# Attention: transposes in tiles of two banks, with the scores put between transposes and value products

## The chip, the core and the metric

The kernel runs on one core of a Trainium2 chip. The metric is the device time of one execution in microseconds. The engines are named as the profile names them: PE (TensorE, matrix products and transposes), DVE (VectorE), ACT (ScalarE), POOL (GpSimd) and SP (SyncE, which issues the DMAs).

## What is computed

One layer of an encoder: a combined input projection, RWKV-7 time mixing on half of the width, stick-breaking attention on the other half, an output projection and a squared-ReLU MLP. The change touches the attention alone:

```python
for blk in range(T // Q_BLOCK):
    z = jnp.einsum('bhqd,bhkd->bhqk', q[:, :, start:end], k[:, :, :end]) * scale
    causal = jnp.arange(end)[None, :] < (start + jnp.arange(Q_BLOCK))[:, None]
    log_beta = jax.nn.log_sigmoid(z)
    log_keep = jnp.where(causal, log_beta - z, 0.0)
    log_a = log_beta + lax.cumsum(log_keep, axis=3, reverse=True) - log_keep
    att = jnp.where(causal, jnp.exp(log_a), 0.0)
    outs.append(jnp.einsum('bhqk,bhkd->bhqd', att, v[:, :, :end]))
```

There are 2048 tokens and 8 attention heads of 64.

## The kernel before

The program runs three stages one after the other: projections with RWKV (stage 1), attention (stage 2), output projection with the MLP (stage 3). In stage 2 the queries stand in four blocks b of 512 and the heads in four pairs hp. For each pair of b and hp, key blocks j of 512 keys are gone through from j=b (the diagonal one) down to j=0. One such (b, hp, j) is a **step**: 40 steps, of which 16 are diagonal and 24 are full. A step has a front and a back.

- `front` (lines 262 to 284), once for each of four query tiles i: PE makes the scores z of both heads (L271; with a mask in a diagonal step, L273), ACT takes two sigmoids of them (`keep`, L275, and `ga`, L277), DVE scans `keep` backwards into E (L281, once for each head), POOL multiplies `ga` by E (L282). There are two z buffers (two PSUM banks each) and two `keep` buffers, nine of `ga` and six of E.
- `back` (lines 285 to 304), once for each of four key tiles kt: PE transposes the 128x128 pieces of `ga` into a PSUM tile `tr`, the tile is copied to SBUF as `th`, and the value products read `th` and add up in OT. A key tile is done in two halves u, of two query tiles each: four transposes into a `tr` of one bank (two buffers), one copy of 512 elements (ACT, L302, or for three of eight DVE, L301), two products (L304). In a diagonal step the pieces above the diagonal are left out.
- `finish` (lines 305 to 313), after the last step of a head pair: DVE copies OT, PE transposes it into `o` (L310, in a buffer of `tr`), ACT copies `o` out (L312) and a DMA stores it.

`step` (lines 316 to 326) issues the front of a new step and the back of the step before it, one tile of each in turn. What order the engines get is set by a scheduler when the program is built: it moves instructions past each other within these dependences, so that fronts can stand up to about a step and a half ahead. Each engine then works through its own list in order, and waits on semaphores.

Stage 3 loads its first data through SP's queue; these loads stand behind the store of the last `osb` (L313).

In names such as `th31210` or `ga3122` the digits are b, hp, j, then the tile, and in `th` and `tr` of the kernel before a last digit u.

Of the kernel before, what the change touches and what calls it, by code (L numbers as in the profile page):

```python
# [8 lines left out]
F32 = mybir.dt.float32  # L9
# [234 lines left out]
def stage2(tc,consts,kd,qd,vd,sbd,cfg=None):  # L244

    nc=tc.nc; V_=nc.vector; A=nc.scalar; P=nc.gpsimd; TE=nc.tensor
    g=dict(GA=9,E=6,TH=4,QB=3,DV=(1,4,7))
    g.update(cfg or {})
    with ExitStack() as ctx:
        sp=ctx.enter_context(tc.tile_pool(name="s2",bufs=1,reuse_waits="tile"))  # L250
# [34 lines left out]
        def back(b,hp,j,gas,OT,kt):  # L285

            n=f"{b}{hp}{j}"; V=kv[hp,j][1]
            i0=kt if j==b else 0; q0=128*i0
            for u in range(2):

                c0=max(i0,2*u)
                if c0>=2*u+2: continue
                tr=pt.tile([128,2,256],F32,tag="tr",name=f"tr{n}{kt}{u}",bufs=2)
                for h in range(2):
                    for i in range(c0,2*u+2):
                        ga,o=gas[i]
                        TE.transpose(tr[:,h,128*(i-2*u):128*(i-2*u)+128],ga[:,h,o+128*kt:o+128*kt+128],consts['ident'])  # L297
                th=sp.tile([128,2,256],F32,tag="th",name=f"th{n}{kt}{u}",bufs=g['TH'])
                q=slice(128*(c0-2*u),256); qq=slice(128*c0,256*u+256)
                cnt[1]+=1  # L300
                if cnt[1]%8 in g['DV']: V_.tensor_copy(out=th[:,:,q],in_=tr[:,:,q])  # L301
                else: A.copy(th[:,:,q],tr[:,:,q])  # L302
                for h in range(2):
                    TE.matmul(OT[64*h:64*h+64,qq],lhsT=V[:,kt,64*h:64*h+64],rhs=th[:,h,q],start=j==b and kt==0 and u==0,stop=j==0 and kt==3 and u==1,skip_group_check=True)  # L304
        def finish(b,hp,OT):
# [3 lines left out]
            o=pt.tile([128,4,128],F32,tag="tr",name="o"+n,bufs=2)  # L309
# [6 lines left out]
        def step(new):  # L316
            prev,late[0]=late[0],new
            for i in range(4):
                if new:
                    b,hp,j,Q,carry,gas,st=new  # L320
                    gas.append(front(b,hp,j,Q,carry,i))
                if prev:
                    b,hp,j,Q,carry,gas,st=prev
                    if j==b and i==0: st.append(pp.tile([128,512],F32,tag="OT",name=f"OT{b}{hp}",bufs=1))
                    back(b,hp,j,gas,st[0],i)
                    if j==0 and i==3: finish(b,hp,st[0])
# [403 lines left out]
```

## Time and profile before

| | us |
|---|---|
| median of 3 runs (3341.51 to 3344.73) | 3343.86 |
| the profiled execution | 3338.49 |
| its span, first to last instruction | 3336.7 |
| attention stage, 1122.9 to 1665.4 of the span | 542.5 |
| PE busy in it | 506.8 |
| DVE busy in it | 397.3 |
| ACT busy in it | 369.2 |
| POOL busy in it | 274.5 |

The page of the profile gives shares over the whole span, in which the attention is a sixth. So the views to read are those cut to this stage: busy time of the engines in a window, the waits of PE there, and the timeline, which shows in order what each engine did and how long it sat idle before. A busy time of PE counts the ends of its products, which run on while the next product starts; the distance between starts is what an instruction occupies.

### The profile page before, as it was taken

What the parts mean: (1) busy time and instruction counts of PE and PEld (TensorE: products, weight loads), DVE (VectorE), ACT (ScalarE), POOL (GpSimd) and SP (SyncE); (2) the same over time, 40 slices, a digit from 0 to 9 for tenths busy, and PEclk for the clock granted to TensorE, in tenths of its full rate; (3) what the DMA queues carried; (4) which work ended last, traced back from release to release, by engine and by line L of the source; (5) the groups of instructions that cost most, each with busy time, mean ns of one, the idle gap of its engine ahead of it and who ended that gap; (6) DMA issues with size and microseconds to landing.
All of it is one profiled execution on the core that took longest, in us unless ns stands there. A gap on an engine that the chain in (4) does not pass through costs nothing. (4 is left out here: it accounts for less than half of the span.)

```text
span 3336.7 us, 45433 instructions
## 1 busy us (share of the span) xinstructions
PE 3166.1 (95%) x17504; PEld 2398.0 (72%) x17504; DVE 2010.7 (60%) x3139; ACT 1167.7 (35%) x2192; POOL 1245.4 (37%) x1089
## 2 busy tenths in 40 slices
PE   8999999999998799999959999999999999999998
PEld 6677767777777544444448788888888888888887
DVE  4674575476375477778566555555555755555555
ACT  4434443443442476667522221111111411111112
POOL 5444444443442354555455432222222422222223
PEclk9999999999998799999979999999999999999999
DMA  3342242232232400000065221111111421111111
GB/s 100 101 120 74 85 131 75 83 121 83 73 100 66 136 23 17 14 10 7 4 199 165 89 76 51 51 45 45 45 51 48 158 79 51 51 45 45 44 44 63
DMA packets 146729, 239.30 MB, mean 72 GB/s; under 512 B 50000, under 2 KB 58192, under 8 KB 146512
## 3 DMA queue, kind: packets, MB, share of 16 engines
q1 hardware_dynamic: 146512, 236.39, 22.7%
q8 instruction: 138, 2.26, 0.3%
q14 instruction: 79, 0.65, 0.1%
HBM read 190.14 MB, written 46.20 MB: 71 GB/s over the span
## 5 line engine op out<-in xcount | busy, mean ns | idle before, releaser
L160 DVE TENSOR_TENSOR acc<-acc,dn 128x512 f32<-128x512 f32 x512 | 344.5, 685 | 411.2 <-PE dn L32 405.6
L282 POOL TENSOR_TENSOR ga<-ga,E 128x1024 f32<-128x1024 f32 (+3 forms) x160 | 274.5, 1726 | 275.6 <-ACT ga L277 124.5
L145 ACT ACTIVATE r<-up 128x512 f32<-128x512 f32 x128 | 75.6, 592 | 615.4 <-PE up L32 615.4
L148 DVE TENSOR_TENSOR m<-r 128x512 f32<-128x512 f32 x128 | 190.9, 1492 | 113.5 <-ACT r L145 113.5
L281 DVE TENSOR_TENSOR_SCAN E<-keep,E,pad 128x513 f32<-128x513 f32 x192 | 232.4, 1263 | 36.4 <-ACT keep L275 36.4
L304 PE MATMUL OT<-th,V 128*64 128x256 f32 (+1 forms) x1152 | 179.5, 392 | 18.2 <-DVE th L301 17.8
L297 PEld LDWEIGHTS tr<-ident,ga 128*128 128x128 f32 x1088 | 114.5, 140 | 105.6 <-issue 94.1
L297 PE MATMUL tr<-ident,ga 128*128 128x128 f32 x1088 | 181.5, 287 | 5.4 <-DVE th L301 2.2
L271 PE MATMUL z<-K,Q 64*128 64x512 f32 (+3 forms) x640 | 159.8, 582 | 11.4 <-DMA Q<-qd 7.7
L275 ACT ACTIVATE keep<-z 128x1024 f32<-128x1024 f32 (+3 forms) x160 | 144.7, 906 | 72.1 <-PE z L273 31.0
L149 DVE TENSOR_TENSOR gl<-m,gh 128x512 fp32r<-128x512 f32 x128 | 148.4, 1160 | 11.6 <-ACT gh L146 0.9
L277 ACT ACTIVATE ga<-z 128x1024 f32<-128x1024 f32 (+3 forms) x160 | 143.7, 904 | 29.1 <-PE tr L297 28.4
L304 PEld LDWEIGHTS OT<-th,V 128*64 128x64 f32 x1152 | 57.6, 134 | 103.4 <-issue 40.1
L302 ACT COPY th<-tr 128x512 f32<-128x512 f32 (+1 forms) x180 | 101.2, 566 | 75.8 <-PE tr L297 74.7
L386 POOL TENSOR_TENSOR wls<-wfs,whs 128x512 fp32r<-128x512 f32 x64 | 84.3, 1318 | 109.1 <-ACT whs L385 100.8
L281 DVE TENSOR_TENSOR_SCAN E<-keep,pad 128x129 f32<-128x129 f32 (+3 forms) x128 | 97.6, 806 | 42.0 <-ACT keep L275 31.1
L535 DVE TENSOR_TENSOR tm<-Am,Xs 128x240 f32<-128x240 f32 (+27 forms) x248 | 106.1, 428 | 23.4 <-DMA Am<-scrA 17.1
L536 DVE TENSOR_TENSOR Xs<-Xs,tm 128x240 f32<-128x240 f32 (+27 forms) x248 | 113.5, 458 | 6.3
L30 PE MATMUL ips<-hT,whs 128*128 128x512 f32 x256 | 108.4, 423 | 0.5 <-ACT whs L385 0.4
L32 PE MATMUL ips<-hT,wls 128*128 128x512 f32 x256 | 107.9, 421 | 0.6 <-POOL wls L386 0.6
L301 DVE COPY th<-tr 128x512 f32<-128x512 f32 (+1 forms) x108 | 69.8, 647 | 63.1 <-PE tr L297 57.9
L30 PE MATMUL op<-wo,yh 128*128 128x512 f32 x256 | 103.4, 404 | 3.3 <-ACT yh L116 3.3
(1265 smaller groups left out, 8675.6 us busy)
## 6 DMA issues: line engine op xcount, KB each, us to landing
wfs<-w_in SPq DMA_DIRECT2D x64, 256.0 KB, 2.9
x<-x SPq DMA_DIRECT2D x32, 256.0 KB, 3.0
wfr<-w_in SPq DMA_DIRECT2D x32, 256.0 KB, 2.7
wfk<-w_in SPq DMA_DIRECT2D x32, 256.0 KB, 2.7
wfv<-w_in SPq DMA_DIRECT2D x32, 256.0 KB, 2.7
wfsv<-w_in SPq DMA_DIRECT2D x32, 256.0 KB, 2.8
x<-x SPq DMA_DIRECT2D x16, 512.0 KB, 3.6
out<-fo SPq DMA_DIRECT2D x32, 256.0 KB, 2.4
```

The lines of the kernel that those rows point to most:

```text
L30: nc.tensor.matmul(ps,lhsT=lh,rhs=rh,start=first,stop=False)
L148: V.tensor_tensor(out=m,in0=r,in1=r,op=ALU.mult)
L149: V.tensor_tensor(out=gl[:,bl],in0=m,in1=gh[:,bl].bitcast(F32),op=ALU.subtract)
L160: V.tensor_tensor(out=a,in0=a,in1=ps,op=ALU.add)
L271: TE.matmul(z[:,h,0:W],lhsT=Q[64*h:64*h+64,128*i:128*i+128],rhs=K[64*h:64*h+64,0:W],start=True,stop=j<b,skip_group_check=True)
L275: A.activation(s[:,:,o:512],z[:,:,0:W],AF.Sigmoid,scale=-0.125)
L277: A.activation(ga[:,:,o:512],z[:,:,0:W],AF.Sigmoid,scale=0.125)
L281: V_.tensor_tensor_scan(E[:,h,o:513][:,::-1],s[:,h,o:513][:,::-1],pad.to_broadcast([128,W+1]),init,ALU.mult,ALU.bypass)
L282: P.tensor_tensor(out=ga[:,:,o:512],in0=ga[:,:,o:512],in1=E[:,:,o+1:513],op=ALU.mult)
L297: TE.transpose(tr[:,h,128*(i-2*u):128*(i-2*u)+128],ga[:,h,o+128*kt:o+128*kt+128],consts['ident'])
L304: TE.matmul(OT[64*h:64*h+64,qq],lhsT=V[:,kt,64*h:64*h+64],rhs=th[:,h,q],start=j==b and kt==0 and u==0,stop=j==0 and kt==3 and u==1,skip_gr ...
L536: V.tensor_tensor(out=X[:,0:m,i+1:],in0=X[:,0:m,i+1:],in1=tm[:,0:m,i+1:],op=ALU.add)
```

## The change

The eight transposes of a key tile go into one `tr` of two banks, of which there is one buffer (before: two of one bank). `th` is as large as `tr`, with two buffers (before: four of half the size). The tile leaves PSUM as follows. In a full key tile with odd kt, ACT copies all of it in one instruction of 1024 elements. With even kt, ACT copies the first half of the columns of each half tile and DVE the second, so that every value product reads what both wrote. On the diagonal with kt=1, ACT copies the part in the first bank and DVE the part in the second; with kt=2 and kt=3, DVE copies alone. In the program's text the front now stands between `turn` (transposes and copies) and `values` (the products) of each tile. The `o` of `finish` uses the one `tr` buffer.

```diff
-    g=dict(GA=9,E=6,TH=4,QB=3,DV=(1,4,7))
+    g=dict(GA=9,E=6,TH=2,QB=3)
...
-            for u in range(2):
-
-                c0=max(i0,2*u)
-                if c0>=2*u+2: continue
-                tr=pt.tile([128,2,256],F32,tag="tr",name=f"tr{n}{kt}{u}",bufs=2)
-                for h in range(2):
-                    for i in range(c0,2*u+2):
-                        ga,o=gas[i]
-                        TE.transpose(tr[:,h,128*(i-2*u):128*(i-2*u)+128],ga[:,h,o+128*kt:o+128*kt+128],consts['ident'])
-                th=sp.tile([128,2,256],F32,tag="th",name=f"th{n}{kt}{u}",bufs=g['TH'])
-                q=slice(128*(c0-2*u),256); qq=slice(128*c0,256*u+256)
-                cnt[1]+=1
-                if cnt[1]%8 in g['DV']: V_.tensor_copy(out=th[:,:,q],in_=tr[:,:,q])
-                else: A.copy(th[:,:,q],tr[:,:,q])
-                for h in range(2):
-                    TE.matmul(OT[64*h:64*h+64,qq],lhsT=V[:,kt,64*h:64*h+64],rhs=th[:,h,q],start=j==b and kt==0 and u==0,stop=j==0 and kt==3 and u==1,skip_group_check=True)
+            def turn():
+
+                tr=pt.tile([128,2,2,256],F32,tag="tr",name=f"tr{n}{kt}",bufs=1)
+                th=sp.tile([128,2,2,256],F32,tag="th",name=f"th{n}{kt}",bufs=g['TH'])
+                for u in range(2):
+                    for h in range(2):
+                        for i in range(max(i0,2*u),2*u+2):
+                            ga,o=gas[i]
+                            TE.transpose(tr[:,u,h,128*(i-2*u):128*(i-2*u)+128],ga[:,h,o+128*kt:o+128*kt+128],consts['ident'])
+                if i0==0:
+
+                    if kt%2: A.copy(th,tr)
+                    else:
+                        A.copy(th[:,:,:,0:128],tr[:,:,:,0:128])
+                        V_.tensor_copy(out=th[:,:,:,128:256],in_=tr[:,:,:,128:256])
+                else:
+                    if i0==1: A.copy(th[:,0,:,128:256],tr[:,0,:,128:256])
+                    q=slice(128*max(i0-2,0),256)
+                    V_.tensor_copy(out=th[:,1,:,q],in_=tr[:,1,:,q])
+                return th
+            def values(th):
+                for u in range(2):
+                    c0=max(i0,2*u)
+                    if c0>=2*u+2: continue
+                    for h in range(2):
+                        TE.matmul(OT[64*h:64*h+64,128*c0:256*u+256],lhsT=V[:,kt,64*h:64*h+64],rhs=th[:,u,h,128*(c0-2*u):256],start=j==b and kt==0 and u==0,stop=j==0 and kt==3 and u==1,skip_group_check=True)
+            return turn,values
...
-            o=pt.tile([128,4,128],F32,tag="tr",name="o"+n,bufs=2)
+            o=pt.tile([128,2,2,256],F32,tag="tr",name="o"+n,bufs=1)[:,0].rearrange("p h (i d) -> p (h i) d",d=128)
...
             for i in range(4):
+                ths=None
+                if prev:
+                    b,hp,j,Q,carry,gas,st=prev
+                    if j==b and i==0: st.append(pp.tile([128,512],F32,tag="OT",name=f"OT{b}{hp}",bufs=1))
+                    turn,values=back(b,hp,j,gas,st[0],i)
+                    ths=turn()
                 if new:
                     b,hp,j,Q,carry,gas,st=new
                     gas.append(front(b,hp,j,Q,carry,i))
                 if prev:
                     b,hp,j,Q,carry,gas,st=prev
-                    if j==b and i==0: st.append(pp.tile([128,512],F32,tag="OT",name=f"OT{b}{hp}",bufs=1))
-                    back(b,hp,j,gas,st[0],i)
+                    values(ths)
```

The order that the scheduler makes of it differs from the text. PE before, in the full step (b=3, hp=1, j=2), key tiles 1 and 2; L297 are transposes, L304 value products:

```order
L297 MATMUL tr31210_14211<-ident_60,ga3120_14086 128x128
L297 MATMUL tr31210_14211<-ident_60,ga3121_14115 128x128
...
L304 MATMUL OT31_14092<-th31201_14197,V12_12479 64x256 x2
L297 MATMUL tr31211_14220<-ident_60,ga3122_14141 128x128
L297 MATMUL tr31211_14220<-ident_60,ga3123_14160 128x128
...
L304 MATMUL OT31_14092<-th31210_14216,V12_12479 64x256 x2
L297 MATMUL tr31220_14239<-ident_60,ga3120_14086 128x128
L297 MATMUL tr31220_14239<-ident_60,ga3121_14115 128x128
...
L304 MATMUL OT31_14092<-th31211_14225,V12_12479 64x256 x2
```

PE now, at the same place (the value products are L314):

```order
L297 MATMUL tr3121_13993<-ident_60,ga3122_13942 128x128
L297 MATMUL tr3121_13993<-ident_60,ga3123_13959 128x128
L314 MATMUL OT31_13880<-th3121_13994,V12_12393 64x256 x4
L297 MATMUL tr3122_14018<-ident_60,ga3120_13897 128x128
L297 MATMUL tr3122_14018<-ident_60,ga3121_13921 128x128
...
L297 MATMUL tr3122_14018<-ident_60,ga3122_13942 128x128
L297 MATMUL tr3122_14018<-ident_60,ga3123_13959 128x128
L314 MATMUL OT31_13880<-th3122_14019,V12_12393 64x256 x4
L297 MATMUL tr3123_14044<-ident_60,ga3120_13897 128x128
```

Before, the products of one half tile came after the transposes of the next one; now the products of a key tile come right after its own transposes, with no scores between at this place. Over the stage, 71 of the 160 key tiles have nothing between their last transpose and their first product: in full steps all 24 with kt=1, all 24 with kt=2, 6 with kt=0 and 2 with kt=3; on the diagonal 7 with kt=2 and 8 with kt=3. In the other 89, one to two scores stand there.

DVE now, around two copies of the full step (3, 1, 0), with the engines whose semaphores an instruction waits for (L303 is DVE's half of the copy of an even key tile, L281 the scan):

```order
L303 COPY th3100_14178<-tr3100_14177 128x4x128 [waits Activation_49]
L281 SCALAR_TENSOR_TENSOR E3221_14340<-keep1_10848,E3231_14224,pad_10851 128x513 [waits Activation_49,Pool_49]
...
L281 SCALAR_TENSOR_TENSOR E3222_14361<-keep0_10847,E3232_14252,pad_10851 128x513 [waits Activation_49,Pool_49]
...
L303 COPY th3102_14233<-tr3102_14232 128x4x128 [waits Activation_49]
L281 SCALAR_TENSOR_TENSOR E3223_14378<-keep1_10848,E3233_14279,pad_10851 128x513 [waits Activation_49,Pool_49]
```

ACT now, at the same place (L300 and L302 are copies, L275 and L277 the sigmoids):

```order
L302 COPY th3100_14178<-tr3100_14177 128x4x128 [waits DVE_49,PE_49]
L275 ACTIVATE keep1_10848<-z3221_14334 128x2x512 [waits DVE_49,PE_49,Activation_49]
L275 ACTIVATE keep0_10847<-z3222_14355 128x2x512 [waits DVE_49,PE_49,Activation_49]
L300 COPY th3101_14206<-tr3101_14205 128x1024 [waits PE_49]
L302 COPY th3102_14233<-tr3102_14232 128x4x128 [waits DVE_49,PE_49]
L277 ACTIVATE ga3221_14338<-z3221_14334 128x1024 [waits PE_49,Pool_49]
L277 ACTIVATE ga3222_14359<-z3222_14355 128x1024 [waits PE_49,Pool_49]
L300 COPY th3103_14261<-tr3103_14260 128x1024 [waits PE_49,Activation_49]
```

DVE's half does not wait for PE but for ACT: the semaphore value is that of ACT's half of the same tile. DVE, before, at the copies of the same step (each waits for PE, and none for ACT):

```order
L301 COPY th31010_14450<-tr31010_14445 128x512 [waits DVE_49,PE_49]
L281 SCALAR_TENSOR_TENSOR E3221_14568<-keep1_10848,E3231_14441,pad_10851 128x513 [waits Activation_49,Pool_49]
...
L301 COPY th31020_14480<-tr31020_14475 128x512 [waits DVE_49,PE_49]
...
L301 COPY th31031_14519<-tr31031_14514 128x512 [waits PE_49]
```

So in an even key tile the two half copies have become a chain, ACT and then DVE. The lists of POOL and SP have the same instructions in the same order as before, and on PE, DVE and ACT nothing has moved outside the attention.

## Rows read from the trace of the kernel before

**Rows 1.** Attention stage: length, busy us of PE, PEld, DVE, ACT, POOL, clock, DMA

```profile
1122.90:1665.40 542.50, 506.77 (x3068) 247.32 (x3068) 397.27 (x444) 369.19 (x515) 274.53 (x160) 0.99 0.09 29
```

**Rows 2.** Waits of PE there: total us, times, longest

```profile
PE OT L304 <- DVE th L301: 17.8, 32, 1.4
PE o L310 <- DVE ots L308: 8.2, 9, 1.1
```

**Rows 3.** Timeline, 1500 to 1508 us: start, us, engine, what [idle before]

```profile
1500.31 0.66 PE L297 MATMUL tr<-ident,ga 128*128 128x128 f32 x4
...
1500.89 0.65 PE L304 MATMUL OT<-th,V 128*64 128x256 f32 x4
1501.00 0.59 ACT L302 COPY th<-tr 128x512 f32<-128x512 f32 x1 [0.58 <-PE tr L297]
...
1501.47 0.66 PE L297 MATMUL tr<-ident,ga 128*128 128x128 f32 x4
...
1503.89 0.66 DVE L301 COPY th<-tr 128x512 f32<-128x512 f32 x1
...
1504.61 0.65 PE L304 MATMUL OT<-th,V 128*64 128x256 f32 x4 [1.31 <-DVE th L301]
...
1505.78 1.13 PE L271 MATMUL z<-K,Q 64*128 64x512 f32 x4
...
1506.84 0.65 PE L304 MATMUL OT<-th,V 128*64 128x256 f32 x4
```

**Rows 4.** Groups by shape in the stage: busy us, mean ns

```profile
L277 ACT ACTIVATE ga<-z 128x1024 f32<-128x1024 f32 x112 | 114.9, 1032 | 22.2 <-PE tr L297 21.9
...
L302 ACT COPY th<-tr 128x512 f32<-128x512 f32 x160 | 93.9, 590 | 73.2 <-PE tr L297 72.2
L301 DVE COPY th<-tr 128x512 f32<-128x512 f32 x96 | 65.0, 677 | 58.7 <-PE tr L297 53.5 <-ACT th L302 4.2
...
L301 DVE COPY th<-tr 128x256 f32<-128x256 f32 x12 | 4.9, 404 | 4.4 <-PE tr L297 4.4
```

**Rows 5.** Timeline of PE: transposes of o that end a head pair

```profile
1148.91 0.66 PE L310 MATMUL o<-ident,ots 128*128 128x128 f32 x4 [0.80 <-DVE ots L308]
...
1186.38 0.63 PE L310 MATMUL o<-ident,ots 128*128 128x128 f32 x4
...
1290.09 0.66 PE L310 MATMUL o<-ident,ots 128*128 128x128 f32 x4 [1.09 <-DVE ots L308]
...
1456.08 0.66 PE L310 MATMUL o<-ident,ots 128*128 128x128 f32 x4 [1.09 <-DVE ots L308]
...
1620.87 0.66 PE L310 MATMUL o<-ident,ots 128*128 128x128 f32 x4 [1.10 <-DVE ots L308]
...
1666.13 0.66 PE L310 MATMUL o<-ident,ots 128*128 128x128 f32 x4 [0.80 <-DVE ots L308]
```

**Rows 6.** Timeline of DVE and of ACT at such a place

```profile
1563.48 7.14 DVE L281 TENSOR_TENSOR_SCAN E<-keep,E,pad 128x513 f32<-128x513 f32 x6
...
1560.96 1.04 ACT L277 ACTIVATE ga<-z 128x1024 f32<-128x1024 f32 x1
1561.91 1.03 ACT L275 ACTIVATE keep<-z 128x1024 f32<-128x1024 f32 x1
```

**Rows 7.** Timeline at the end of the stage: SP's queue

```profile
1667.43 0.36 SPq L313 DMA_DIRECT2D sbd<-osb  x1
1667.84 0.50 SPq L69 DMA_DIRECT2D gnw<-gnw  x1
```

**Rows 8.** Busy time of PE and its granted clock in two stretches

```profile
159.00:165.00 6.00, 5.82 (x13) 0.50 0.50 142
...
1286.00:1292.00 6.00, 4.32 (x24) 1.00 0.00 0
```

**Rows 9.** Timeline of PE: at half clock as the stage starts; masks later

```profile
1130.97 0.76 PE L297 MATMUL tr<-ident,ga 128*128 128x128 f32 x3
...
1589.87 0.44 PE L273 MATMUL z<-cmask,identr 128*128 128x128 f32 x2
```

## Prediction

> **What bounds the kernel now.** I read first the busy times cut to the attention, since the change touches nothing else. In its 542.5 us PE is busy 506.8, DVE 397.3, ACT 369.2 and POOL 274.5 [rows 1]: PE is the bound, and little of its time is empty. Second, the waits of PE there: 17.8 us in 32 pieces at the value products, put down to DVE's copies, and 8.2 at the `o` of a finished head pair [rows 2]. That is what a better order could win. Third, the timeline, to see why there is so little. Four transposes take 0.58 us of PE (1500.31 to 1500.89), four value products as much (1500.89 to 1501.47), a score of full width 1.06 (1505.78 to 1506.84) [rows 3]. ACT's copy of a half tile begins 0.11 us after the transposes have been issued and lasts 0.59 (1501.00 to 1501.59) [rows 3]. While it runs, PE does the products of the half tile before and the transposes of the next one, 1.17 us together, so nothing is lost. Where a copy is late PE stops at once: the copy that ended at 1504.55 let the products start at 1504.61, after 1.31 us of nothing [rows 3]. The gap shows the return trip too, 0.06 us.
>
> **What stands against each stretch.** The starts of `o` mark the ends of head pairs [rows 5]. They give the time of a pair: 12.5 us in block 0 (37.5 for three), 25.9 in block 1 (103.7 for four), 41.5 in block 2 (166.0 for four), 54.9 in block 3 (164.8 for three), and 45.3 for the last, which has no fronts of a next pair beside it. A full step without any gap is eight half tiles, each 0.58 of transposes and 0.58 of products, and four scores at 1.06: 13.6 us. A diagonal step is 11.0: 20 transposes 2.9, products of six half tiles 3.1, scores of one to four quarters of the width 2.7, eight masks 1.5 (two last 0.44 [rows 9], less the 0.07 by which a product runs on beside the next one), and `o` with what the short scores take more than their share, 0.8 by estimate. A pair of block 3, one diagonal and three full steps, would take 51.8 us, so it loses 3.1 now.
>
> **What the change takes away.** The same 1088 transposes, products and scores remain; PE's own work is unchanged. ACT has 52 copies fewer and DVE four more, of other sizes. ACT and DVE are not the bound [rows 1], so I put that at nothing by itself. The overlap by half tiles goes: the products of a key tile now follow its own transposes, and the one `tr` buffer forbids the next transposes until the copies are done. What can cover a copy is only a score, and at 71 of 160 places the order has none.
>
> **What an uncovered copy costs.** A copy of 1024 elements by ACT isn't in the trace; the nearest row is a sigmoid of the same shape from the same two banks, 1.03 us [rows 4]. I take that: 0.11 + 1.03 + 0.06 = 1.2 us at an odd key tile. Bounds: two copies of 512, 2 x 0.59 [rows 4], make 1.35; one of them, were the second bank free of charge, 0.76. At an even key tile DVE's half waits for ACT's semaphore, as the order shows, so the halves add up: 0.11 + 0.59 + 0.1 from engine to engine + 0.68 [rows 4] + 0.06 = 1.5 us. Were they side by side, it would be 0.85. On the diagonal DVE copies alone: 0.85 at kt=2 (0.68 of copy), 0.6 at kt=3 (0.40 [rows 4]).
>
> The Trainium skill, "PSUM — Partial Sum Buffer", section "PSUM bank collisions raise a hardware error", says that two engines must not access one bank on the same partitions at once, reads included. That speaks against halves copied at once from the same banks, and the semaphore in the order agrees with it; no row here shows two engines on one bank. By that rule 1.5 stands, without it 0.85.
>
> The 71 bare places: 24 x 1.2 (kt=1) + 24 x 1.5 (kt=2) + 6 x 1.5 + 2 x 1.2 + 7 x 0.85 + 8 x 0.6 = 28.8 + 36 + 9 + 2.4 + 6 + 4.8 = **87 us**.
>
> **What stands behind queues at the covered places.** Scores that used to be spread over a step now come in bursts of up to five at the end of one step and the start of the next. DVE takes 1.19 us for a scan (7.14 for six [rows 6]), so 2.4 for each score, against PE's 1.06, and its list is in order: a copy put behind two scores' scans waits for them. I walked one pair of block 3 through the four lists, with these durations, sigmoids at about 0.9 from start to start [rows 6], two z buffers that come free when ACT has read them, and two `keep` buffers that come free when DVE has scanned them. Time zero is the last key tile of the last full step of the pair before:
> - around the end of the pair: 0.5 us before its scores, 0.35 and 1.2 at `o` (its OT copy stands behind two scans), 1.6 at the fourth score (no z buffer: ACT waits for `keep`, which waits for DVE), 2.4 at the first products of the diagonal step (DVE's half behind six scans), 0.6 at a score, then 1.2 and 0.6 at the last two diagonal tiles: 8.4 us;
> - the first full step: 0.5, 1.2, 1.5 and 0.5 (scores wait for `ga` buffers that the last transposes free): 3.7;
> - the second: 0.3, 1.2, 1.5: 3.0;
> - the third: 1.2 (two scores' scans ahead of DVE's half), 1.2, 1.5: 3.9.
>
> That is 19.0 us of gaps on 51.8 of work, 70.8 instead of 54.9: **+15.9** a pair. The last pair has 41.0 of work, having no fronts of a next pair, and two full steps without any score (1.5 + 1.2 + 1.5 + 1.2 = 5.4 each): gaps of 8.4 + 3.7 + 2 x 5.4 = 22.9, 63.9 instead of 45.3, **+18.6**. The same walk gives 54.0 in block 2 (7.0 + 5.0 + 3.8 of gaps on 38.2), 32.6 in block 1 and 15.1 in block 0: +12.5, +6.7 and +2.6 a pair.
>
> **The sum.** 3 x 15.9 + 18.6 + 4 x 12.5 + 4 x 6.7 + 4 x 2.6 = 47.7 + 18.6 + 50 + 26.8 + 10.4 = **+153.5 us**. Nothing gives it back later: stage 3's first loads stand in SP's queue behind the last store of the attention (1667.43, then 1667.84 [rows 7]), so all of stage 3 moves by the same amount. Seen the other way: 87 us at bare places, about 103 behind queues, less some 37 of idle time that is there today and is counted anew. Against the profiled execution 3338.5 + 153.5 = **3492 us**, 4.6% slower. The median of the runs lies 5.4 us above that execution, which is small beside the uncertainty; about 0.2% is what a measurement can tell from no change.
>
> **Rivals.**
> - *Only the bare places, and halves side by side.* If DVE's backlog costs no more than now, and the halves overlap in effect, the bare places cost 24 x 1.2 + 24 x 0.85 + 6 x 0.85 + 2.4 + 6 + 4.8 = 67.5, and the 17.8 us of today's waits on copies [rows 2] go: +50, 3388 us. For it: today's DVE has the same bursts in places and PE loses only 3 us a pair. Against it: the semaphore in the order, and today PE has the other half tile to do meanwhile. Chance 0.14; with the halves in a chain but no backlog it is 3338.5 + 87 - 17.8 = 3408.
> - *The scores do stand between, in effect: faster.* If copies end within what lies between transposes and products, the waits on copies vanish, and fewer and longer copies leave ACT more room. What can go is the 17.8 us [rows 2]: 3338.5 - 17.8 = 3321 us. It decides from the point where a copy takes less than the score beside it, 1.06 us, and all tiles have a score; the order has it at 89 of 160. Chance 0.04. That the gains and losses meet within 0.2%: 0.03.
> - *The clock falls.* PE would be idle a quarter of the stage. In stage 1 the granted clock was 0.50 through a stretch of 6 us; in the attention it stayed at 1.00 through one of 6 us with PE busy 4.32 [rows 8], 72%, which is about what the walk leaves it. At half clock, 1.2 of 2.4 GHz, a transpose takes 0.25 us (0.76 for three [rows 9]) instead of 0.15. One such stretch of 6 us in each full step, with PE at work for 72% of it and doing 0.58 of the work, would cost 6 x 0.72 x 0.42 = 1.8 us, 24 times: +44 on the sum, 3536 us. It decides from the point where the clock doesn't hold at that share. Chance 0.12.
>
> The Trainium skill, "TensorE: Matmul & The Clock Gate", section "Part 4: PE-mode transpose", says that transposes don't count as work for the clock as products do. By that rule the third rival would come true in the steps without scores, whose products alone would have to hold the clock; the stage as it is, with more than a thousand transposes, has 0.99 on average [rows 1], which doesn't bear it out.
>
> **How the numbers follow.** The walk, 3492 us, has 0.67, with 3430 to 3540 as its own range: real waits are as likely to be a little longer than walked (semaphores between each) as a backlog is to be shorter (scans that start earlier than I took them). The first rival 0.14, the clock 0.12, faster 0.04, no change 0.03. The range from 3400 to 3550 takes in the walk, the chain without backlog at 3408 and the clock's point at 3536; it leaves out the first rival's lower part, the two small cases and a clock worse than walked, together about 0.2. Faster by over 0.2% has 0.04, within 0.2% 0.03, slower 0.93.
>
> **What the profile after should show.** The attention stage about 695 us long with the same busy time of PE to within some 10 us, so PE idle for some 180; waits of PE at L314 on DVE as the largest, in more than 60 pieces, with ACT's second; gaps of 1.5 us after the transposes of even key tiles and of 1.2 after odd ones in the last two steps, where nothing else runs; DVE's L303 starting 0.1 us after ACT's L302 has ended, and never beside it; the clock at 1.00; stages 1 and 3 as long as before. I am wrong if L303 runs beside L302, if gaps at first products on the diagonal stay under 1 us (then the backlog was overdrawn), or if the clock drops within the stage.

## The result and the profile after

The changed kernel takes 3510.0 us (median of 4 runs, 3507.2 to 3517.6) against 3343.6 for the kernel before in the same session: a ratio of 1.050, with a 95% interval from 1.0485 to 1.0521. That is 166 us slower, where 153.5 had been forecast; 3510 lies in the range, 18 us above the point.

The first view is again the busy time cut to the attention (length, then busy us of PE, PEld, DVE, ACT and POOL, then the granted clock). The changed kernel:

```profile
1127.70:1836.70 709.00, 515.79 (x3071) 275.45 (x3072) 402.21 (x448) 366.44 (x463) 274.82 (x160) 0.94 0.07 22
```

The same view of the kernel before, with the ends of the stage set in the same way (first score to last transpose of `o`; [rows 1] stop 1.1 us earlier):

```profile
1122.90:1666.50 543.60, 507.14 (x3071) 247.69 (x3072) 397.95 (x444) 369.19 (x515) 274.53 (x160) 0.99 0.09 29
```

The stage grew by 165.4 us. PE's busy time grew by 8.7, so its idle time went from 36.5 to 193.2 us. DVE, ACT and POOL are busy as before, to within 5 us: none of them got more to do, and PE waits for them. The clock fell from 0.99 to 0.94; the trace's record of the granted clock has 91 us at half in the stage, where before it was 8.6, all at the stage's start. From the last `o` to the end both kernels take 1670 us: nothing is given back. The 4.7 us by which the stage begins later are not the change's: the kernels below, equal in stage 1, begin it anywhere from 1122.9 to 1131.4.

PE's waits in the attention of the changed kernel (total us, times, longest), to hold against [rows 2]:

```profile
PE OT L314 <- DVE th L303: 74.4, 56, 2.1
PE z L271 <- ACT ga L277: 47.7, 72, 1.7
PE OT L314 <- ACT th L300: 29.6, 27, 1.2
PE OT L314 <- DVE th L307: 17.6, 30, 2.4
PE o L321 <- DVE ots L319: 14.5, 13, 1.6
```

Before, the value products waited 17.8 us in 32 pieces; now it is 121.6 in 113. Counted place by place in the trace, the 71 key tiles with nothing between have 84 us of this, the other 89 have 38. The scores wait too, 47.7 us, for ACT to read a z buffer; before it was 3.3.

The timeline of the changed kernel in the last pair shows one even key tile without scores, one odd one with a score, and an even one with DVE's scans in the way (start, us, engine, what, idle before and its cause):

```profile
1799.49 1.09 PE L297 MATMUL tr<-ident,ga 128*128 128x128 f32 x8
1800.62 0.59 ACT L302 COPY th<-tr 128x512 f32<-128x512 f32 x1 [2.20 <-PE tr L297]
1801.24 0.69 DVE L303 COPY th<-tr 128x512 f32<-128x512 f32 x1 [2.70 <-ACT th L302]
...
1801.99 1.08 PE L314 MATMUL OT<-th,V 128*64 128x256 f32 x8 [1.40 <-DVE th L303]
...
1804.72 1.13 PE L271 MATMUL z<-K,Q 64*128 64x512 f32 x4 [0.63 <-ACT ga L277]
...
1805.47 1.02 ACT L300 COPY th<-tr 128x1024 f32<-128x1024 f32 x1
...
1806.54 1.08 PE L314 MATMUL OT<-th,V 128*64 128x256 f32 x8 [0.69 <-ACT th L300]
...
1807.52 2.46 DVE L281 TENSOR_TENSOR_SCAN E<-keep,E,pad 128x513 f32<-128x513 f32 x2 [5.59 <-ACT keep L275]
...
1808.69 0.59 ACT L302 COPY th<-tr 128x512 f32<-128x512 f32 x1 [0.35 <-PE tr L297]
1809.89 0.67 DVE L303 COPY th<-tr 128x512 f32<-128x512 f32 x1
...
1810.62 1.08 PE L314 MATMUL OT<-th,V 128*64 128x256 f32 x8 [1.97 <-DVE th L303]
```

At the first, ACT's half ends at 1801.21 and DVE's begins at 1801.24; PE stands for 1.40 us. At the last, ACT's half ends at 1809.28 but DVE is in its scans until 1809.89, and PE stands for 1.97. The 1024-element copy, which no row of before had, takes 1.02 us.

The clock falls where PE has waited long: nine of its twelve falls after the stage's start stand at a wait of over 2 us for a copy of DVE, the other three at a wait of 1.1 us for `ots` at the end of a pair. PE of the changed kernel right after the end of block 1, and the busy times (columns as above) just before and just after the fall:

```profile
1339.63 1.09 PE L297 MATMUL tr<-ident,ga 128*128 128x128 f32 x8
1342.39 1.13 PE L271 MATMUL z<-K,Q 64*128 64x512 f32 x4 [1.67 <-ACT ga L277]
1345.62 1.97 PE L314 MATMUL OT<-th,V 128*64 128x256 f32 x8 [2.10 <-DVE th L303]
1347.53 1.54 PE L297 MATMUL tr<-ident,ga 128*128 128x128 f32 x6
```

```profile
1340.00:1345.00 5.00, 1.85 (x11) 0.78 (x9) 5.00 (x6) 3.44 (x4) 4.00 (x2) 0.97 0.25 74
1345.00:1362.00 17.00, 15.27 (x62) 8.74 (x62) 7.91 (x12) 4.49 (x7) 4.63 (x3) 0.51 0.03 10
```

DVE is busy for all of the five us before the fall: PE waits because DVE is behind. Then the diagonal step runs at half clock, eight value products in 1.91 us from start to start instead of 1.02.

### The profile page after: what moved, and what is told of

Same layout as the page of the kernel before. It is cut to its first block, busy times and chain, and to the rows that moved or that the text cites. A ratio compares the mean times of both kernels' runs of the same rounds, so it can differ in the third digit from the quotient of the medians.

```text
span 3506.3 us, 45382 instructions
## 1 busy us (share of the span) xinstructions
PE 3172.2 (90%) x17504; PEld 2423.6 (69%) x17504; DVE 2018.8 (58%) x3143; ACT 1165.5 (33%) x2140; POOL 1246.3 (36%) x1089
## 5 line engine op out<-in xcount | busy, mean ns | idle before, releaser
L282 POOL TENSOR_TENSOR ga<-ga,E 128x1024 f32<-128x1024 f32 (+3 forms) x160 | 274.8, 1727 | 430.5 <-ACT ga L277 344.6
L281 DVE TENSOR_TENSOR_SCAN E<-keep,E,pad 128x513 f32<-128x513 f32 x192 | 232.8, 1264 | 104.7 <-ACT keep L275 101.8
L314 PE MATMUL OT<-th,V 128*64 128x256 f32 (+1 forms) x1152 | 165.2, 404 | 121.9 <-DVE th L303 74.4
L271 PE MATMUL z<-K,Q 64*128 64x512 f32 (+3 forms) x640 | 166.4, 610 | 55.3 <-ACT ga L277 47.7
L314 PEld LDWEIGHTS OT<-th,V 128*64 128x64 f32 x1152 | 70.5, 142 | 210.6 <-DVE th L303 101.9
L277 ACT ACTIVATE ga<-z 128x1024 f32<-128x1024 f32 (+3 forms) x160 | 142.3, 903 | 114.6 <-PE tr L297 114.6
L297 PEld LDWEIGHTS tr<-ident,ga 128*128 128x128 f32 x1088 | 125.0, 148 | 76.8 <-issue 65.4
L275 ACT ACTIVATE keep<-z 128x1024 f32<-128x1024 f32 (+3 forms) x160 | 144.9, 906 | 97.8 <-DVE E L281 24.6
L297 PE MATMUL tr<-ident,ga 128*128 128x128 f32 x1088 | 165.7, 295 | 9.0 <-POOL ga L282 5.9
L281 DVE TENSOR_TENSOR_SCAN E<-keep,pad 128x129 f32<-128x129 f32 (+3 forms) x128 | 96.6, 805 | 74.9 <-ACT keep L275 64.7
L271 PEld LDWEIGHTS z<-K,Q 64*128 64x128 f32 x640 | 51.6, 197 | 98.2 <-ACT ga L277 81.3
L30 PE MATMUL ips<-hT,whs 128*128 128x512 f32 x256 | 108.8, 425 | 0.6 <-ACT whs L401 0.5
L31 PE MATMUL ips<-hT,whs 128*128 128x512 f32 x256 | 105.2, 411 | 0.0
```

The lines of the kernel that those rows point to most:

```text
L30: nc.tensor.matmul(ps,lhsT=lh,rhs=rh,start=first,stop=False)
L31: nc.tensor.matmul(ps,lhsT=lh,rhs=rl,start=False,stop=False)
L271: TE.matmul(z[:,h,0:W],lhsT=Q[64*h:64*h+64,128*i:128*i+128],rhs=K[64*h:64*h+64,0:W],start=True,stop=j<b,skip_group_check=True)
L275: A.activation(s[:,:,o:512],z[:,:,0:W],AF.Sigmoid,scale=-0.125)
L281: V_.tensor_tensor_scan(E[:,h,o:513][:,::-1],s[:,h,o:513][:,::-1],pad.to_broadcast([128,W+1]),init,ALU.mult,ALU.bypass)
L282: P.tensor_tensor(out=ga[:,:,o:512],in0=ga[:,:,o:512],in1=E[:,:,o+1:513],op=ALU.mult)
```

## The experiments

Four theories stood against each other. **A**: a copy costs what PE has nothing to put beside it, and more where DVE's copy stands behind scans. **B**: the one buffer of two banks costs by itself, wherever the scores and products stand. **C**: it is the bursts of scores. **D**: a part of it is the clock. An order "pinned" below is an order of instructions on PE alone, with no wait added.

**e1_adj.** The kernel before, its half tiles and copies untouched, but each half tile's transposes pinned behind the products of the half tile before:

```diff
-                        TE.transpose(tr[:,h,128*(i-2*u):...],ga[:,h,o+128*kt:o+128*kt+128],consts['ident'])
+                        t=TE.transpose(tr[:,h,128*(i-2*u):...],ga[:,h,o+128*kt:o+128*kt+128],consts['ident'])
+                        if lastv[0] is not None: behind(tc,t,lastv[0])
...
-                    TE.matmul(OT[64*h:64*h+64,qq],...)
+                    lastv[0]=TE.matmul(OT[64*h:64*h+64,qq],...)
```

> The kernel before with its tiles and copies as they are (half tiles, two tr buffers, four th); only on PE the transposes of a half tile stand behind the products of the half tile before, so products follow their own transposes. By its order 177 of 288 half tiles then have nothing between. Theory A (a copy costs what PE has nothing to put beside it): 177 x about 0.8 us (0.75 for ACT's copies, 0.9 for DVE's) = 140 us more, about 3480. Theory B (the single tr buffer of the change is what costs, the place of the products doesn't matter): no change, about 3340. Theory C (bursts of scores are what costs): within 20 us of before.

Measured: 3679.4 us, ratio 1.100 (1.095 to 1.106). The direction is A's, the size is not: some 200 us more. The stage, and a stretch of 28 us in it:

```profile
1612.00:1640.00 28.00, 23.68 (x92) 11.77 (x90) 5.90 (x9) 7.06 (x12) 4.63 (x3) 0.50 0.00 1
1131.40:2016.40 885.00, 663.55 (x3071) 305.31 (x3072) 403.27 (x444) 377.98 (x515) 275.25 (x160) 0.78 0.05 18
```

PE does the same work as before and is busy 156 us longer, because 397 us of the stage are at half clock. In the second half of the stretch shown, four transposes, a gap of 0.7 us and four products alternate, and the clock stays at half, though PE is busy for 23.68 of 28 us by the slow clock. The loss is A's gaps (idle 221 us instead of 36), and the clock nearly doubles it (D).

**e2_lag.** The changed kernel's tiles and copies, but the products of a key tile pinned one key tile later, behind the next transposes (`pay` issues the products of the tile before, m is such a product):

```diff
-                    values(ths)
+                pay(); due[0]=nxt
...
+                        behind(tc,m,lastt[0])
```

> The changed kernel with its tiles, buffers and copies as they are; only the products of a key tile stand behind the transposes of the next key tile. Theory A: the products of the tile before (1.17 us) cover most of a copy (1.2 or 1.5), so the 87 us at bare places shrink to about 15, and copies that are late by DVE's backlog are partly covered: 3390 to 3430. Theory B: the next transposes still wait for the copies in the one buffer, about 3500. Theory C: the bursts of scores stay, about 3490.

Measured: 3437.5 us, ratio 1.028 (1.025 to 1.031), 7 us above A's span and far from B's and C's. The products no longer wait for copies; the next transposes do, for the one `tr`:

```profile
PE tr L301 <- DVE th L307: 69.6, 48, 4.4
PE o L326 <- DVE th L307: 26.1, 15, 3.1
PE tr L301 <- DVE th L311: 21.7, 13, 2.4
```

The order is worth 73 us. The other 94 stay: the one `tr` buffer makes the next transposes wait for copies, and a part of these copies is late by DVE's scans (the longest wait is 4.4 us). So B has a share, which this run doesn't part from DVE's backlog.

**e3_banks.** The changed kernel, but each bank a tile of its own, with its own copy; who copies goes by bank, and the order is the scheduler's:

```diff
-                tr=pt.tile([128,2,2,256],F32,tag="tr",bufs=1)
-                th=sp.tile([128,2,2,256],F32,tag="th",bufs=g['TH'])
+                    tr=pt.tile([128,2,256],F32,tag=f"tr{u}",bufs=1)
+                    th[u]=sp.tile([128,2,256],F32,tag=f"th{u}",bufs=g['TH'])
...
+                    if i0==0 and (kt%2 or u==0) or i0==1 and u==0: A.copy(th[u][:,:,q],tr[:,:,q])
+                    else: V_.tensor_copy(out=th[u][:,:,q],in_=tr[:,:,q])
```

> The changed kernel with the two banks as two tiles of one bank each (tr and th alike), in full key tiles ACT copying the first and DVE the second with even kt, ACT both with odd kt; amounts of copying per engine as in the changed kernel, order left to the scheduler. Theory A: with a buffer for each half the products can again stand half a tile behind, so nearly all of the loss goes: 3340 to 3370. Theory B: tr holds no more than before the split, but each half comes free by itself: some gain, 3440. Theory C: scores come in bursts still, about 3420.

Measured: 3340.6 us, ratio 0.9987 (0.9973 to 1.0002): the loss is gone. The stage is 543.2 us long with PE busy 503.7. As long as a bank is a tile, the scheduler lays products of one half beside the copy of the other.

**e4_bankadj.** e3_banks with the transposes of a key tile pinned behind all products of the one before, which is the changed kernel's order without its tile:

```diff
+                            if lastv[0] is not None: behind(tc,t,lastv[0])
...
-                        TE.matmul(OT[64*h:64*h+64,128*c0:...],...)
+                        lastv[0]=TE.matmul(OT[64*h:64*h+64,128*c0:...],...)
```

> As with the two banks as two tiles, but on PE the transposes of a key tile stand behind all products of the key tile before, as in the changed kernel. So it tells the chain of the two half copies from the place of the products. Theory A: the first half's copy starts beside the second half's transposes and the halves don't wait for each other; a bare place costs about 0.3 us instead of 1.2 to 1.5: the 87 us become 20, and some of the backlog stays: 3410 to 3450. Theory B: about 3440 too. Theory C: about 3490.

Measured: 3432.9 us, ratio 1.027 (1.023 to 1.030). That is in A's span, but B's number, about 3440, is as near, so the time alone does not tell the two apart. Half of the loss returns with the order alone.

```profile
PE z L275 <- ACT ga L281: 41.6, 47, 2.7
PE OT L315 <- DVE th L308: 31.6, 47, 1.2
PE OT L315 <- ACT th L307: 15.5, 56, 0.6
```

DVE's half no longer waits for ACT's: where DVE is not in its scans, it begins 0.2 us before ACT's copy has ended. The products of the first half now start on the first copy alone, and those of the second wait again for the second, here at key tile 2 of a full step with DVE in its scans until shortly before:

```profile
1641.08 0.65 PE L315 MATMUL OT<-th,V 128*64 128x256 f32 x4 [0.29 <-ACT th L307]
...
1642.00 0.65 PE L315 MATMUL OT<-th,V 128*64 128x256 f32 x4 [0.27 <-DVE th L308]
```

Counted place by place, the 56 bare places of full steps cost 22.9 us in all, 0.41 each, against 0.3 and 20 expected; in the changed kernel they cost 1.1 to 1.7 each. The rest of the waits of the last two lines lies on the diagonal and at covered places. So most of what the order brings back is not at the bare places: the scores wait 41.6 us for z (3.3 before), and 75 us of the stage are at half clock.

**e5_scan.** The changed kernel with the scans of the second head left out, so that half of the weights' computation is missing and DVE has 148 us less to do:

```diff
-            for h in range(2):
+            for h in range(1):
...
-            P.tensor_tensor(...,in1=E[:,:,o+1:513],op=ALU.mult)
+            P.tensor_tensor(...,in1=E[:,0:1,o+1:513].to_broadcast([128,2,W]),op=ALU.mult)
```

> The changed kernel with the scans of the second head left out: POOL multiplies both heads by the first head's E, so DVE has half its scans (some 136 us of 402 less) and half the computation of the weights is missing. Theory A (a copy costs what PE has nothing to put beside it, plus DVE's copies that stand behind scans): the backlog on DVE goes and the bare places stay, 3415 to 3445 us, with the waits of PE on L303 down from 74 us to about 50. If DVE's queue is the whole loss: 3350 to 3375. If DVE's queue costs nothing: 3490 to 3515.

Measured: 3417.1 us, ratio 1.022 (1.019 to 1.026): A. The stage, and PE's waits:

```profile
1122.90:1746.40 623.50, 482.52 (x3072) 259.85 (x3072) 254.41 (x288) 362.96 (x463) 274.09 (x160) 0.99 0.08 25
```

```profile
PE z L271 <- ACT ga L277: 45.7, 73, 1.1
PE OT L314 <- DVE th L303: 44.8, 38, 1.4
PE OT L314 <- ACT th L300: 29.6, 27, 1.2
PE OT L314 <- DVE th L307: 9.4, 15, 0.8
```

Without the backlog of scans no gap at an even tile is longer than 1.4 us, at an odd one than 1.2. What is left on the products is 44.8 + 29.6 + 9.4 = 83.8 us in 80 pieces; about 80 us of it lie at the 71 bare places. The scores' waits stay at 45.7, so they are not DVE's. They go with the bursts, two z buffers against up to five scores in a row: e6_spread, below, has no bursts and none of these waits. So C has a share too, some 42 us over the 3.3 of before. DVE's queue accounts for at least 52 us of PE's idle time (193.2 less 141.0; half of the scans are still there), and for most of the time at half clock: 13.8 us instead of 91. On PE the two kernels have the same instructions in nearly the same order, so the difference in busy time gives the price of half clock: (515.8 - 482.5) / (91.2 - 13.8) = 0.43 us for each us at half. e1_adj against the kernel before gives 156.4 / 388.3 = 0.40.

**e6_spread.** The changed kernel's tiles, but one score pinned between the transposes and the products of every key tile t (`ahead` issues one front, six tiles ahead, and `pay` the products). Two more `ga` buffers go with it, eleven instead of nine:

```diff
+        for t in range(160):
+            turn,values=back(b,hp,j,gas,None,t%4)
+            nxt=(made[t//4],t%4,values,turn())
+            ahead(t+6)
+            due[0]=nxt; pay()
```

> The changed kernel's tiles and copies, but one score pinned between the transposes and the products of every key tile (the fronts run six key tiles ahead, with two more ga buffers), so that there is no bare place and no burst. Theory A: a score covers 1.06 us, so 0.1 us is left at odd key tiles and 0.45 at even ones, 48 each, and about 10 on the diagonal: 3345 + 5 + 22 + 10 = 3380, between 3365 and 3400, with the clock at 1.00 for nearly the whole stage. Theory B (the one buffer of two banks costs by itself, wherever the scores stand): 3460 to 3510. If scores in between are worth more than the copies cost, as the change's name has it: below 3340.

Measured: 3415.4 us, ratio 1.022 (1.019 to 1.025), between the spans of A and B. Where DVE is free it comes out as costed:

```profile
1509.73 1.13 PE L275 MATMUL z<-K,Q 64*128 64x512 f32 x4
...
1509.83 0.59 ACT L307 COPY th<-tr 128x512 f32<-128x512 f32 x1 [1.25 <-PE tr L302]
1510.45 0.69 DVE L308 COPY th<-tr 128x512 f32<-128x512 f32 x1 [0.84 <-ACT th L307]
...
1511.20 1.08 PE L319 MATMUL OT<-th,V 128*64 128x256 f32 x8 [0.34 <-DVE th L308]
```

The score covers all but 0.34 of the 1.40. But DVE's copies still stand behind the scans of the scores that come at the same rate: the waits on DVE's copies are 47.0 and 36.8 us, and 48 us are at half clock. The change's idea, a score in between, recovers 95 us when it is done at every tile, and the tile still loses 70. What the two more `ga` buffers do by themselves was not run.

**e7_fillM and e8_fillT.** The changed kernel with work for nothing on PE at 48 bare places, four products or eight transposes, to keep the clock up; the column of zeros that the scans read gave up its PSUM bank for it:

```diff
-        pad=pp.tile([128,1],F32,name="pad"); V_.memset(pad,0.0)
+        pad=sp.tile([128,1],F32,name="pad"); V_.memset(pad,0.0)
+        fl=pp.tile([128,512],F32,name="fl")
...
+                if i0==0 and kt in (1,2):
+                    for r in range(4):
+                        m=TE.matmul(fl,lhsT=kv[hp,j][0][:,0:128],rhs=kv[hp,j][0],start=True,stop=True)
```

> The changed kernel with work for nothing in its gaps: after the transposes of key tiles 1 and 2 of a full step (48 places) PE does four products of 64 us's kind, K by K, 512 columns wide, into a bank of its own that nobody reads, about 1.06 us, before it comes to the value products; the column of zeros that the scans read moves out of that bank. Added work some 51 us, nothing taken away. Theory D (about a fifth of the loss is the clock, which falls to half when PE has been idle and then slows the dense diagonal step): half clock falls from 91 us of the stage to under 20, 3460 to 3485 us. Rival (half clock costs nothing, since PE waits for copies anyway): 3505 to 3540.

> As e7_fillM, with eight transposes of the identity into the same bank in the place of the four products, about 1.02 us. If transposes hold the granted clock as products do: 3460 to 3485 us, as e7_fillM. If transposes do nothing for the clock: half clock stays at 90 us or more, a filler of 2 us at half clock is then longer than the gap it stands in, 3510 to 3545.

Measured: 3735.8 and 3647.9 us, both far outside every span. Neither answers its question, since the moved column was no small thing:

**e9_pad.** The changed kernel with the column moved to SBUF and nothing else (the first two lines of the diff above).

> The changed kernel with one line moved: the column of zeros that every scan reads lies in SBUF instead of PSUM, as in e7_fillM and e8_fillT, and there is no filler. If the column is what slowed those two (their scans took 1.8 us on the mean instead of 1.2, twice as long beside POOL's multiplications): 3580 to 3650 us. If the fillers did it: 3500 to 3520.

Measured: 3652.3 us, ratio 1.092 (1.087 to 1.096). So the column alone did what e8_fillT showed, and e8's transposes cost nothing beside it; e7's products cost 84 us more, being longer than the gaps (3.53 us a place from start to start, where 1.06 had been expected). Held against e9_pad, the two fillers still say something: the stage has 304 us at half clock without a filler, 270 with the transposes and 241 with the products, so neither kept the clock up. DVE's scans in this kernel:

```profile
L281 DVE TENSOR_TENSOR_SCAN E<-keep,E,pad 128x513 f32<-128x513 f32 x192 | 322.3, 1727 | 103.2 <-ACT keep L275 103.2
```

In the changed kernel the same 192 scans take 1264 ns each, in the kernel before 1263. DVE's backlog grows with them. As a test of theory A this serves after all: 114 us more of DVE's time made the stage 141 us longer, by the clock too, although DVE is busy for only 516 of 850 us.

**e10_actall.** The changed kernel with every full key tile copied whole by ACT:

```diff
-                    if kt%2: A.copy(th,tr)
-                    else:
-                        A.copy(th[:,:,:,0:128],tr[:,:,:,0:128])
-                        V_.tensor_copy(out=th[:,:,:,128:256],in_=tr[:,:,:,128:256])
+                    A.copy(th,tr)
```

> The changed kernel, but ACT copies every full key tile whole; DVE keeps only the diagonal's. Theory A: an even place costs 1.2 instead of 1.5 us (30 bare ones, 9 us), and 48 copies leave DVE's list, where they stand behind scans: the 74 us of waits on L303 shrink to what a copy by ACT costs, 3440 to 3480 us. Rival (ACT, with 20 us more of work and the sigmoids in the same list, is as late as DVE was): 3495 to 3530, with the waits of scores on ACT above 60 us.

Measured: 3459.1 us, ratio 1.034 (1.030 to 1.038): A. Four lines become one, and 51 us of the loss are gone:

```profile
PE OT L311 <- ACT th L300: 64.3, 57, 1.4
PE z L271 <- ACT ga L277: 50.4, 70, 1.7
```

A place costs 64.3 / 57 = 1.13 us, with no chain of two engines and no scans ahead (the 56 bare places of full steps have 63.5 us of it); the products' waits are 83 us in all instead of 121.6.

**e11_best and e12_bestA.** What the runs had shown, put together: a bank is a tile (e3), the products stand one key tile behind (e2), one score in every key tile, with eleven `ga` buffers (e6). e12 also lets ACT copy all full tiles (e10).

```diff
-            due[0]=nxt; pay()
+            pay(); due[0]=nxt
```

and in e12_bestA, beside it:

```diff
-                    if i0==0 and (kt%2 or u==0) or i0==1 and u==0: A.copy(th[u][:,:,q],tr[:,:,q])
+                    if i0==0 or i0==1 and u==0: A.copy(th[u][:,:,q],tr[:,:,q])
```

> The tiles of e3_banks, one score pinned after the transposes of every key tile, and the products one whole key tile behind: eight transposes in a row, a score, eight products of the tile before. Theory A: copies have 2.1 us of PE's work beside them, so waits on copies stay at some 20 us, and rows of eight of a kind (1.02 us) in the place of two of four (2 x 0.58) save up to 0.14 x 192 = 27 us of PE: 3315 to 3340 us, faster than both kernels. Rival (DVE, at four fifths of the stage and in order, is behind with its copies wherever they stand): 3350 to 3390.

> As e11_best, with every copy of a full key tile by ACT, so that DVE has only scans and the diagonal's copies there. Theory A: no copy stands behind a scan, 3310 to 3335 us, and no slower than e11_best. Rival (ACT's list of copies and sigmoids is late instead, so that scores wait for their z buffers): 3345 to 3375.

Measured: 3301.8 us, ratio 0.987 (0.984 to 0.990), and 3299.2, ratio 0.987 (0.983 to 0.990). Both are faster than both kernels, by more than was expected; between them there is nothing to choose. The stage of e11_best, and PE in it:

```profile
1125.10:1634.20 509.10, 482.01 (x3072) 262.50 (x3072) 402.41 (x448) 361.12 (x511) 275.78 (x160) 0.98 0.10 31
```

```profile
1507.32 1.09 PE L305 MATMUL tr<-ident,ga 128*128 128x128 f32 x8
1508.34 1.13 PE L275 MATMUL z<-K,Q 64*128 64x512 f32 x4
1509.40 1.08 PE L315 MATMUL OT<-th,V 128*64 128x256 f32 x8
1510.41 1.09 PE L305 MATMUL tr<-ident,ga 128*128 128x128 f32 x8
```

PE has no gap in this stretch (in the whole stage it waits 22.7 us for DVE's copies), and it is also busy 25 us less than in the kernel before, for the same products. A row of eight transposes takes 1.02 us from start to start (1507.32 to 1508.34) and a row of eight products 1.01; before, four took 0.58, so two rows of four take 1.16 [rows 3]. Two changes of kind are saved in each key tile. Which of the four parts put together is worth what was not run.

## Why the prediction held, point by point

- **The bound, and where the loss goes.** Right: PE idle 193.2 us, forecast 180; DVE's and ACT's busy time unchanged; products' waits on DVE the largest, in 56 pieces at L303 and 30 at L307; L303 starting right behind L302 (0.03 us in the row, forecast 0.1); stage 3 simply later.
- **The bare places, 87 us.** Right: the 71 places have 84 us in the changed kernel itself, and about 80 in e5_scan, where the backlog is gone. The odd place, 1.2 us by the estimate from a sigmoid's row, has 29.6 / 27 = 1.10 of idle time. The even one, 1.5, has 1.40: halves in a chain, as the semaphore in the order said. The prediction took the chain as a sign of its rule on two engines at one bank. It isn't one. On the diagonal with kt=1 ACT and DVE copy from two different banks of the tile, and there too DVE's copy never begins before ACT's has ended. In eight of the 16 steps DVE has nothing else to do and waits for ACT alone:

```profile
DVE th L307 <- ACT th L305: 11.2, 8, 1.7
```

So the chain goes with the tile. Whether halves of one bank could be copied at once, no run shows. Both gaps are 0.1 under the cost, since a part of it is the end of the last transpose, which counts as busy.

- **The queues, about 103 us.** Right in sum, 193.2 - 84 = 109 with what was idle before. Its parts can be told apart now: the backlog of scans some 52 (e5_scan), the scores' waits for z some 46, the rest at `o` and at the stage's first load. The walk put the longest wait for z down to DVE; e5_scan shows that only little of these waits is DVE's. At the first products of a pair the gap is 2.1 us in block 3 (walked 2.4), 1.3 to 2.1 in block 2 and nothing in blocks 0 and 1.
- **The walk.** Pairs of block 1 take 32.5 us (three of four; forecast 32.6), of block 3 70.5, 69.5 and 70.5 (70.8), of block 0 15.1, 17.8 and 15.2 (15.1), the last pair 62.2 (63.9). Block 2 was forecast with 54.0 and took 57.8, 54.9, 57.8 and 54.9. The transposes of `o` that bound two of these, and the busy times of the two pairs:

```profile
1450.68 0.65 PE L321 MATMUL o<-ident,ots 128*128 128x128 f32 x4 [1.10 <-DVE ots L319]
...
1508.47 1.10 PE L321 MATMUL o<-ident,ots 128*128 128x128 f32 x4 [1.10 <-DVE ots L319]
...
1563.35 0.66 PE L321 MATMUL o<-ident,ots 128*128 128x128 f32 x4 [1.10 <-DVE ots L319]
```

```profile
1450.70:1508.50 57.80, 42.58 (x233) 22.90 (x233) 30.72 (x34) 28.23 (x36) 21.20 (x13) 0.85 0.03 10
1508.50:1563.40 54.90, 40.20 (x233) 21.55 (x233) 30.68 (x34) 28.25 (x36) 21.16 (x13) 0.91 0.03 10
```

The same instructions, 2.9 us apart, 2.4 of it in PE's busy time, and the clock differs: 0.85 against 0.91. That blocks 1 and 3 come so near is in part luck, since the two errors below lie in them and offset each other: in the pair from 1563.35 on, 6.8 us at half clock cost some 2.9, and 12 full tiles in rows of eight give back some 3.4.

- **"PE's own work is unchanged": wrong.** It fell. The walk took 0.58 for every four transposes; in the changed kernel they come in eights, at 1.02. With the 96 tiles of full steps, each with one row of eight transposes and one of eight products, that is 96 x 2 x 0.14 = 27 us less (the diagonal, where rows grow too, left out). e5_scan, in nearly the same order and with the clock at 0.99 as before, is in fact busy 24.6 us less, 482.5 instead of 507.1. [rows 3] held only fours, but the diagonal of the kernel before has twos, which I didn't read (its timeline of PE):

```profile
1221.20 0.44 PE L297 MATMUL tr<-ident,ga 128*128 128x128 f32 x2
1221.57 1.13 PE L271 MATMUL z<-K,Q 64*128 64x512 f32 x4
```

Two transposes take 0.37 from start to start, four 0.58: 0.11 for each and about 0.14 once, so eight would come to 1.0.

- **"The clock at 1.00": wrong.** A drop within the stage is one of the prediction's own signs of being wrong. It was a rival at 0.12, and it came true, in another place than walked: not in every full step, but mostly where DVE's backlog stops PE, six times at the first products of a pair. At 0.43 us each the 91.2 us at half clock cost 39, 35 more than before. The two errors nearly cancel in PE's busy time: -27 + 35 = 8, measured 8.7. That is luck: the forecast of an unchanged busy time holds in number, not in reason. With both terms put in, the sum is 3338.5 + 153.5 - 27 + 35 = 3500; the changed kernel's profiled execution took 3508, 4.7 of the difference being the stage's later start.
- **Rivals.** "Only the bare places, halves side by side" falls with the chain and the backlog. Its 0.85 has no run: with the banks as tiles (e4_bankadj) the bare places of full steps cost 0.41 each, since the first half's copy and products no longer wait for the second half. "The scores do stand between" falls at 71 places, and e6_spread shows that it would not have been a gain for this tile even at all 160.

What stays open: which activity of PE lets the clock fall or brings it back. The fillers that were to tell products from transposes were spoilt by the moved column, and neither held the clock up. The Trainium skill ("TensorE: Matmul & The Clock Gate", section "HAM oscillation — how this bites in real kernels") describes work in bursts with waits between, where each burst starts slow again, and counts half of the throttled time as lost. The traces agree with the first in part: the changed kernel's clock falls 12 times after the start of the stage, while PE waits 113 times at its value products alone. For the second they have 0.40 and 0.43 of the time; in the twelve stretches PE is busy for 72.4 of 81.8 us, and half of that share is 0.44.

## What to carry to other kernels

In this build a tile is the unit in which waits are kept: two banks in one tile put the copies of two engines in a chain and, with one buffer, hold the next transposes until the last copy is done. So make a tile of each bank that an engine copies by itself, and give the bound engine one whole tile of other work behind each transpose. Before a change that makes PE wait, ask what its gaps do to the clock, and whether an engine that is busy only 60% of the time is late at the moments that count. Rows of eight instructions of one kind are cheaper on PE than two rows of four, and worth having if an order can be found that hides the copies.

## What the runs showed of the chip

- **Changes of kind cost PE 0.14 us.** Four transposes, or four value products, take 0.58 us when another kind follows; eight take 1.02, two 0.37. In the medians over the stage, where PE does not wait in between, it is 0.58 to 0.59, 1.01 to 1.02 and 0.37. That is about 0.11 each and 0.14 for the change. It holds for eight transposes into two tiles as well as into one (e4_bankadj, e11_best).
- **The busier stretch had the lower clock.** In e1_adj PE was busy for 23.68 of 28 us, as it counts at the slow clock, and the clock was 0.50 throughout; in the kernel before it was 1.00 with 4.32 of 6 [rows 8].
- **A column of zeros adds 37% to a scan.** With it in PSUM a scan takes 1264 ns, in SBUF 1727 on the mean. The Trainium skill, "SBUF — State Buffer", section "Who interferes with whom", says that a DVE instruction with two SBUF inputs contends with a GpSimd instruction that reads SBUF. The runs agree: only the scan's second input was moved, and POOL's own busy time in the stage rose from 274.8 to 308.2 us. In e9_pad's trace one waits for the other: a scan with no multiplication beside it takes 1.25 us, as in the changed kernel. One that begins first takes 1.25 too, and the multiplication started 0.25 us into it takes 2.8 instead of 2.0. One that begins 0.93 us into such a multiplication, at 1482.4, takes 2.96 and ends 1.08 us after it.
